# Copies of the value windows in long runs in later blocks, and the transposes of the chunk inverses 22 products later, in a transformer layer on one core

## The chip, the cores and the metric

The kernel runs on one core of a Trainium2 chip. The metric is the device time of one execution in microseconds (us). Before the change the median of 3 runs is 1508.61 us (1508.04 to 1511.2).

## The reference

One layer of a diffusion backbone: 1024 latent tokens and 256 context tokens, width 1024. After modulation and RMS norm, one input projection feeds two groups of heads: a gated DeltaNet (group A, 4 heads of 128, scanned forward and backward) and a neighbourhood attention (group B, 8 heads of 64, windows of 8 rows by 32 gathered columns on a grid of 64 columns). Both go through an output projection and a SwiGLU feed-forward. What matters here:

```python
# group A: q, k, v of the short convolution; one chunk of the scan needs the inverse of a unit triangle
m = jnp.where(strict, jnp.einsum("bhncd,bhnmd->bhncm", kb, k) * decay, 0.0)
a_mat = jnp.eye(CHUNK, dtype=f32) + m
u = lax.linalg.triangular_solve(a_mat, v * beta[..., None], left_side=True, lower=True, unit_diagonal=True)
w = lax.linalg.triangular_solve(a_mat, kb * jnp.exp(gam)[..., None], left_side=True, lower=True, unit_diagonal=True)
...
# group B: normalised queries and keys, values of a window of columns
q = rms_norm(q, q_norm_w) * NA_HEAD_DIM ** -0.5
k = rms_norm(k, k_norm_w)
...
v_r = lax.dynamic_slice_in_dim(vg, r0, win_rows, axis=1)[:, :, key_cols]
```

## The kernel before

Every number is kept as a pair of a rounded value and its rest (hh and hl for the activations, whi and wlo for the weights), and a product of two such pairs is three matmuls on TensorE (PE). The input projection is computed in blocks of 128 columns. The list `jobs` holds them in order: k0 to k3 and a wide block; from `inv` on nk0, nk1, nk2, a wide block, nk3 (keys of group B); nq0, nq1, nq2 (its queries), q0; from `turn` on q1, q2, q3 (queries of group A), v0 to v3, nq3; from `gates` on z0 to z3. A block goes through eight steps k, each with hh by whi, hl by whi and hh by wlo, for two segments of 512 tokens (nq, q, z: 48 products of 128 x 512) or for 256 + 512 + 512 tokens (k, nk, v). Each block has its weights loaded by SyncE (SP) one block ahead (L218), cast to whi by ScalarE (ACT, L219) and subtracted to wlo by GpSimd (POOL, L221); whi and wlo have two buffers, wraw one. At its end ACT evacuates the PSUM banks into `cacc` (L491), of which there are two.

`norm()`, called one block later, does for nk and nq blocks: products of the squares with a block matrix (m<-cr,cst and pr<-cr,cst, L548), Ln and Exp on ACT (L549 to L553, each with a load of its function table), the scaling by VectorE (DVE, L556), a cast to half precision on ACT (L561 for nk, L568 for nq), the subtraction for its rest on DVE (L562, L569), and stores to nk_d or nq_d (L574).

Beside the blocks a generator, `bg`, is stepped once per k before `turn` and three times after. It yields after small pieces of work:

- `block_inverses()` inverts 32 x 32 triangles: a recursion of 60 DVE steps over the matrix N (L947, L949), the diagonal set (L952), one yield, then 32 transposes of N on PE into PSUM banks `m` (written at L957 and recorded at L106, the line of the helper), eight copies from them to WK on DVE (L961), and for both directions a 32 x 32 transpose (L967), a store to x_d, a scaling (L970) and another store (L972).
- `preps()` then makes 20 preparations, one per direction and chunk of 128 tokens, up to three in flight. One loads e, kk and xc (xc from x_d; L997 to L999), copies xc into fx on ACT (L1011) and into y on POOL, takes exponentials of e on ACT (L1015), multiplies kk by e on DVE (L1016), and then does four dependent groups of products on PE: pr<-fx,kk, whose result ACT copies back (L1028), and three of pr<-y,kk, each of which needs the copy on DVE of the one before it (L1036).

A third generator, `copies`, is added after the wide block 8 and stepped twice per k: `windows()` copies the values' columns of four overlapping windows from nv_d to vw_d in DRAM, 16 copies of 256 KB in runs of 2 KB, on SP's queue (L1095). The attention, behind the input projection, loads vw from vw_d (L331).

PE, ACT, DVE, POOL and SP each run their instructions in order. A scheduler decides this order when the program is built, from priorities that follow the program's text and from when operands are ready; it can move an instruction between blocks. Where an engine waits, all that stands behind it in its order waits too.

Of the kernel before, what the change touches and what calls it, by code (L numbers as in the profile page):

```python
# [9 lines left out]
F32 = mybir.dt.float32  # L10
# [4 lines left out]
OP = mybir.AluOpType  # L15
# [12 lines left out]
NU = NCH * NH  # L28
# [63 lines left out]
def hybrid(ctx, tc, a, dbg):  # L92
# [75 lines left out]
    vw_d = dram.tile([128, 4, 4, 512], F32, name="vw_d", tag="vw_d")  # L168
# [130 lines left out]
    def attention(nw):  # L299
# [28 lines left out]
        def values(hp, half, cb):  # L328
            if (hp, cb) not in blocks:
                vw = nw.tile([128, 4, 128], F32, name="vw", tag="vw", bufs=3)  # L330
                sp.dma_start(vw, vw_d[:, cb, :, hp * 128:hp * 128 + 128])  # L331
                blocks[hp, cb] = vw
            return blocks[hp, cb][:, half:half + 3]
# [87 lines left out]
    with ExitStack() as bs:  # L421
# [32 lines left out]
        class Block:  # L454
# [79 lines left out]
            def norm(self):  # L534

                kind, acc, t0, i = self.kind, self.acc, self.t0, self.i
                if kind in "vz":
                    return
                if kind == "k":
                    sp.dma_start(kT_d[:, i], acc)  # L540
                    return
                r = self.r
                if kind == "q":
                    sp.dma_start(qT_d[:, i], acc[:, t0:])
                    return
# [8 lines left out]
                isk = kind == "nk"  # L554
# [332 lines left out]
        def block_inverses():  # L887
            with ExitStack() as gs:
# [75 lines left out]
                for d in range(2):  # L964
                    ud = U[:, d * NU:(d + 1) * NU]
                    ut = g4.tile([128, NU, 32], F32, name="ut", tag="ut")
                    dve.transpose(fl(ut), fl(ud))  # L967
                    x, s = (ut, ud) if d else (ud, ut)
                    sp.dma_start(x_d[:, d, 0], x)
                    dve.tensor_tensor(s, s, NB[:, d].rearrange("p c (h o) -> p (c h) o", o=1).to_broadcast(  # L970
                        [128, NU, 32]), OP.mult)
                    sp.dma_start(x_d[:, d, 1], s)  # L972
                    yield

        done = set()

        def preps():

            first_half.close()
            with ExitStack() as gs:  # L980
# [11 lines left out]
                def fetch(d, c):  # L992
# [6 lines left out]
                    sp.dma_start(xc, x_d[:, d, :, c * 4:c * 4 + 4])  # L999
# [56 lines left out]
                n = 0  # L1056
                while live or todo or landing:
# [27 lines left out]
        values = inv + 3  # L1085
# [5 lines left out]
        def windows():  # L1091
            vlat = nv_d[CT:].rearrange("(r c) d -> r c d", c=64)
            for cb in range(4):
                for ch in range(4):
                    sp.dma_start(vw_d[:, cb, ch], vlat[4 * ch:4 * ch + 4, BLKS[cb]:BLKS[cb] + 32])  # L1095
                    yield
# [12 lines left out]
        first[0].norm()  # L1109
        first[1].silu()  # L1110
        for n in range(2, len(jobs) + 2):
# [28 lines left out]
            if isinstance(j, Wide):  # L1140
                for t, _ in enumerate(j.tiles()):
# [15 lines left out]
            elif j:  # L1157
                for k in range(KT):
# [12 lines left out]
            if isinstance(j, Wide) and n == values:  # L1171
                copies.add(windows())
            if nrm:
                nrm.norm()
# [689 lines left out]
```

## Time and profile before

| what | value |
|---|---|
| median of 3 runs | 1508.61 us |
| the profiled execution | 1507.78 us |
| its span, first to last instruction | 1506.0 us |
| PE busy | 1449.8 us |
| mean granted clock of PE | 0.994 |
| places of nk3's end, nq0, nq1 and nq2 in the span | about 250 to 308 us |

The profile comes from one execution. A row of a timeline has the start in us from the span's start, the duration, the engine, the line, the operation, output and inputs by the program's names, sizes and count; in brackets stands the idle time of the engine before it and what ended that. In the windows each engine's busy time is followed by the count of instructions, then come the granted clock of PE (1.00 is full), the busy share of the DMA engines and GB/s.

### The profile page before, as it was taken

What the parts mean: (1) busy time and instruction counts of PE and PEld (TensorE: products, weight loads), DVE (VectorE), ACT (ScalarE), POOL (GpSimd) and SP (SyncE); (2) the same over time, 40 slices, a digit from 0 to 9 for tenths busy, and PEclk for the clock granted to TensorE, in tenths of its full rate; (3) what the DMA queues carried; (4) which work ended last, traced back from release to release, by engine and by line L of the source; (5) the groups of instructions that cost most, each with busy time, mean ns of one, the idle gap of its engine ahead of it and who ended that gap; (6) DMA issues with size and microseconds to landing.
All of it is one profiled execution on the core that took longest, in us unless ns stands there. A gap on an engine that the chain in (4) does not pass through costs nothing.

```text
span 1506.0 us, 23093 instructions
## 1 busy us (share of the span) xinstructions
PE 1449.8 (96%) x8365; PEld 1201.0 (80%) x8365; DVE 1004.4 (67%) x1892; ACT 696.2 (46%) x1321; POOL 193.4 (13%) x223
## 2 busy tenths in 40 slices
PE   5999998899999999999989999999999999999998
PEld 2789787678877778887877878888888888888887
DVE  4886579455598427679966499666655557698642
ACT  6443461584266526566742374333333334354440
POOL 0154500343124221211100000000000000000000
PEclk9999999999999999999999999999999999999999
DMA  9377133555377799986349106333333334898742
GB/s 368 117 234 239 57 92 121 191 168 190 118 243 238 220 284 265 262 228 193 110 134 332 72 30 203 113 105 105 102 102 105 106 105 161 287 349 286 240 145 84
DMA packets 198851, 267.35 MB, mean 178 GB/s; under 512 B 15232, under 2 KB 106960, under 8 KB 197712
## 3 DMA queue, kind: packets, MB, share of 16 engines
q1 hardware_dynamic: 198016, 265.49, 54.7%
q8 instruction: 66, 1.08, 0.3%
q14 instruction: 49, 0.40, 0.1%
q10 hardware_dynamic: 720, 0.37, 0.1%
HBM read 201.01 MB, written 68.98 MB: 179 GB/s over the span
## 4 chain that ended last, share of the span: by engine, by line
PE 51%; DVE 6%; ACT 3%; DMA 2%; issue 1%; SPq 0%; ACTq 0%; DVEq 0%
PE ps L102 45%; PE sc L102 5%; PE sc L106 2%; DMA wad<-wa 1%; ACT pt L377 1%; ACT ex L365 1%; DVE ex L363 1%; DVE acc L255 1%; DVE x L1618 1%; DVE x L1594 0%; DVE ex L367 0%; DVE ulo L1449 0%; DVE lT L1589 0%; DVE ws L1444 0%; ACT x L1598 0%
## 5 line engine op out<-in xcount | busy, mean ns | idle before, releaser
L102 PE MATMUL ps<-hT,uhi 128*128 128x512 f32 x496 | 146.8, 390 | 0.8 <-DVE e L1739 0.7
L102 PE MATMUL ps<-lT,uhi 128*128 128x512 f32 x496 | 146.4, 389 | 0.0
L102 PE MATMUL ps<-hT,ulo 128*128 128x512 f32 x496 | 146.3, 389 | 0.0
L102 PE MATMUL blk<-hh,whi 128*128 128x512 f32 (+1 forms) x456 | 138.0, 393 | 2.4 <-ACT hh L748 1.7
L102 PE MATMUL blk<-hh,wlo 128*128 128x512 f32 (+1 forms) x456 | 129.7, 377 | 0.0
L102 PE MATMUL ps<-hB,uhi 128*128 128x512 f32 x436 | 129.1, 390 | 0.0
L102 PE MATMUL blk<-hl,whi 128*128 128x512 f32 (+1 forms) x456 | 129.0, 376 | 0.0
L102 PE MATMUL ps<-lB,uhi 128*128 128x512 f32 x436 | 128.8, 389 | 0.0
L102 PE MATMUL ps<-hB,ulo 128*128 128x512 f32 x436 | 128.8, 389 | 0.0
L1448 ACT CAST uhi<-ws 128x512 fp32r<-128x512 f32 x91 | 54.7, 622 | 145.5 <-PE ps L102 78.2
L1448 ACT CAST uhi<-wq 128x512 fp32r<-128x512 f32 x101 | 60.4, 621 | 132.8 <-PE ps L102 69.4
L1449 DVE TENSOR_TENSOR ulo<-wq,uhi 128x512 fp32r<-128x512 f32 x101 | 67.1, 687 | 65.6 <-ACT uhi L1448 36.4
L102 PEld LDWEIGHTS ps<-hT,uhi 128*128 128x128 f32 x496 | 93.0, 188 | 20.7 <-ACT uhi L1448 1.1
L102 PEld LDWEIGHTS ps<-lT,uhi 128*128 128x128 f32 x496 | 93.0, 188 | 19.7 <-DVE lT L1602 0.5
L102 PEld LDWEIGHTS ps<-hT,ulo 128*128 128x128 f32 x496 | 93.1, 188 | 19.4
L102 PEld LDWEIGHTS ps<-hB,uhi 128*128 128x128 f32 x436 | 81.8, 188 | 17.5 <-issue 0.5
L102 PEld LDWEIGHTS ps<-lB,uhi 128*128 128x128 f32 x436 | 81.8, 188 | 17.3 <-DVE lB L1602 0.4
L102 PEld LDWEIGHTS ps<-hB,ulo 128*128 128x128 f32 x436 | 81.8, 188 | 17.0
L102 PEld LDWEIGHTS blk<-hh,wlo 128*128 128x128 f32 x456 | 80.1, 189 | 17.6 <-issue 1.7
L102 PEld LDWEIGHTS blk<-hl,whi 128*128 128x128 f32 x456 | 80.7, 189 | 15.5
L102 PEld LDWEIGHTS blk<-hh,whi 128*128 128x128 f32 x456 | 76.5, 189 | 19.8 <-ACT hh L748 3.7
L1449 DVE TENSOR_TENSOR ulo<-ws,uhi 128x512 fp32r<-128x512 f32 x91 | 60.6, 685 | 36.2 <-ACT uhi L1448 28.0
(341 smaller groups left out, 3026.0 us busy)
## 6 DMA issues: line engine op xcount, KB each, us to landing
wq<-w_fo SPq DMA_DIRECT2D x99, 256.0 KB
wq<-w_gu SPq DMA_DIRECT2D x88, 256.0 KB
wad<-wa SPq DMA_DIRECT2D x64, 256.0 KB
t_d<-g SPq DMA_DIRECT2D x22, 512.0 KB
fr<-t_d SPq DMA_DIRECT2D x44, 256.0 KB
bt<-rpb SPq DMA_DIRECT2D x48, 192.0 KB
f_d<-g SPq DMA_DIRECT2D x33, 256.0 KB
fr<-f_d SPq DMA_DIRECT2D x33, 256.0 KB
```

The costliest lines, as they stand in the source:

```text
L102: i = nc.tensor.matmul(*args, **kw)
L106: i = nc.tensor.transpose(*args, **kw)
L255: dve.scalar_tensor_tensor(acc2, x, sc, acc2, op0=OP.mult, op1=OP.add)
L363: dve.tensor_tensor_reduce(ex, sc, bt, 1.0, -3.0e38, OP.add, OP.max, m[:, 0:1])
L365: act.activation(ex, ex, AF.Exp, bias=m[:, 1:2], accum_out=m[:, 2:3])
L377: act.copy(pt, sc)
L1448: act.copy(hi, self.raw[key])
L1449: dve.tensor_tensor(lo, self.raw[key], hi.bitcast(F32), OP.subtract)
L1618: dve.tensor_tensor(B[at][:, k], B[x][:, k], B.get(y, B["B11"])[:, k], OP.subtract)
```

## The change

Four things are changed.

1. vw_d is laid out by window, and `windows()` makes 4 copies of 1 MB, 16 runs of 64 KB each, in program order, one in each of the blocks q2, q3, v0 and v1 (at k = 4).
2. The inverses' transposes come after eight yields instead of one. They are kept in program order; their copies, both 32 x 32 transposes and both scalings get a higher priority. The buffer `ut` becomes a part of N.
3. `norm()` ends after the Exp and returns its second half (`split`: scaling, cast, subtraction, stores). For nk3 this half is issued behind the inverses' last scaling, after block 11's products; for other blocks before `turn` it is issued behind the inverses as well, once they exist.
4. `preps()` fetches the first two chunks ahead and yields three times, and after `turn` `bg` is stepped four times at k = 7.

The core of the diff:

```diff
-    vw_d = dram.tile([128, 4, 4, 512], F32, name="vw_d", tag="vw_d")
+    vw_d = dram.tile([4, 512, 512], F32, name="vw_d", tag="vw_d")
...
-                sp.dma_start(vw, vw_d[:, cb, :, hp * 128:hp * 128 + 128])
+                sp.dma_start(vw, vw_d[cb].rearrange("(n p) d -> p n d", p=128)[:, :, hp * 128:hp * 128 + 128])
...
-                isk = kind == "nk"
+                return self.split
+
+            def split(self):
+
+                acc, t0, i, r = self.acc, self.t0, self.i, self.r
+                isk = self.kind == "nk"
...
-                for _ in range(1):
+                for _ in range(8):
                     yield
                 U = WK.rearrange("p d u i -> p (d u) i")
                 for i0 in range(0, 32, 4):
                     p = bank()
                     for i in range(4):
-                        pe.transpose(p[:, i * P:(i + 1) * P], N[:P, :, :, i0 + i].rearrange("p b r -> p (b r)"),
-                                     ident[:P, :P])
-                    dve.tensor_copy(U[:, :, i0:i0 + 4], p[:, :4 * P].rearrange("p (i u) -> p u i", i=4))
+                        tc.keep_in_program_order(nc.tensor.transpose(
+                            p[:, i * P:(i + 1) * P], N[:P, :, :, i0 + i].rearrange("p b r -> p (b r)"),
+                            ident[:P, :P]))
+                    with tc.high_priority(offset=400):
+                        dve.tensor_copy(U[:, :, i0:i0 + 4], p[:, :4 * P].rearrange("p (i u) -> p u i", i=4))
...
-                    ut = g4.tile([128, NU, 32], F32, name="ut", tag="ut")
+                        ut = N.rearrange("p b r c -> p (b r c)")[:, d * 1280:(d + 1) * 1280].rearrange(
+                            "p (u i) -> p u i", i=32)
...
+                inverse[:] = [end]
+                yield
...
+                landing += [[fetch(*todo.pop(0)), False] for _ in range(2)]
+                for _ in range(3):
+                    yield
...
-                for ch in range(4):
-                    sp.dma_start(vw_d[:, cb, ch], vlat[4 * ch:4 * ch + 4, BLKS[cb]:BLKS[cb] + 32])
-                    yield
+                tc.keep_in_program_order(nc.sync.dma_start(
+                    vw_d[cb].rearrange("(r c) d -> r (c d)", c=32),
+                    vlat[:, BLKS[cb]:BLKS[cb] + 32].rearrange("r c d -> r (c d)")))
+                yield
...
-                    bg.step(1 if n < turn else 3)
+                    bg.step(1 if n < turn else 4 if k == 7 else 3)
                     bg2.step(1)
-                    copies.step(2)
+                    if k == 4:
+                        copies.step(1)
+                if waiting:
+                    while not started:
+                        bg.step(1)
+                    with tc.issue_after(inverse[0].ins):
+                        waiting.pop()()
                 j.evac()
...
-            if isinstance(j, Wide) and n == values:
+            if n == turn:
                 copies.add(windows())
             if nrm:
-                nrm.norm()
+                rest = nrm.norm()
+                if nrm is tail and not inverse:
+                    waiting.append(rest)
+                else:
+                    with tc.issue_after(inverse[0].ins) if inverse and n < turn else ExitStack():
+                        rest()
```

The order on the engines, at the three places that the prediction speaks of. First PE at the transposes (m<-cst,N). Before, they stand in block nq0, from its 33rd product on, among single products (numbers behind hh, hl are those of the activations' tiles; what a row waits for stands in brackets):

```order
L102 MATMUL blk<-hh_417,wlo 128x512 x2
L102 MATMUL blk<-hh_419,whi 128x512 x2
L106 MATMUL m<-cst,N 128x80 [waits DVE_49]
L106 MATMUL m<-cst,N 128x80
L102 MATMUL blk<-hl_420,whi 128x512 x2
L102 MATMUL blk<-hh_419,wlo 128x512
```

After, they stand in the next block, nq1, behind its first six products (tiles 136 and 137 are a block's first):

```order
L102 MATMUL blk<-hh_136,whi 128x512 x2
L102 MATMUL blk<-hl_137,whi 128x512 x2
L102 MATMUL blk<-hh_136,wlo 128x512 [waits Pool_49]
L102 MATMUL blk<-hh_136,wlo 128x512
L964 MATMUL m<-cst,N 128x80 [waits DVE_49,Activation_49]
L964 MATMUL m<-cst,N 128x80
L964 MATMUL m<-cst,N 128x80 [waits DVE_49]
L964 MATMUL m<-cst,N 128x80
```

The last 16 products of nq0, nk3's norm products and six products of nq1 now stand ahead of the first transpose; the rest of the transposes follows in groups of eight with six products between. The first preparation's product (pr<-fx,kk) moves in the same way, in block nq2, from behind 26 products to behind 42.

Second, ACT ahead of the first preparation (fx<-xc). Before, from the Exp of nk3 on:

```order
L553 ACTIVATE cr<-cr 128x1280 [waits Activation_49]
L561 CAST hl_2526<-cacc 128x1280 [waits DVE_49]
L219 CAST whi<-wraw 128x1024 [waits DMAHW3_49,PE_49,Pool_49]
L491 ACTIVATE cacc<-blk 128x512 [waits DVE_49,PE_49]
L491 ACTIVATE cacc<-blk 128x512 [waits PE_49]
L549 ACT_TABLE_LOAD
L549 ACTIVATE cr<-m,bias 128x512 [waits PE_49] x2
L532 ACTIVATE cr<-cacc 128x1024 [waits Activation_49]
L551 ACT_TABLE_LOAD
L551 ACTIVATE cr<-cr,bias 128x1024 [waits Activation_49]
L1011 COPY fx_2478<-xc 32x4x32 [waits DMAHW2_49,Pool_49]
```

After, from the same Exp on (lines are five higher here and ten higher from L1006 on):

```order
L553 ACTIVATE cr<-cr 128x1280 [waits Activation_49]
L219 CAST whi<-wraw 128x1024 [waits DMAHW2_49,PE_49,Pool_49]
L549 ACT_TABLE_LOAD
L549 ACTIVATE cr<-m,bias 128x512 [waits PE_49] x2
L551 ACT_TABLE_LOAD
L551 ACTIVATE cr<-cr,bias 128x1024 [waits Activation_49]
L566 CAST hl_2552<-cacc 128x1280 [waits DVE_49]
L573 CAST hl_2570<-cacc 128x512 [waits DMAHW6_49,DMAHW5_49,DMAHW7_49,DMAHW4_49,DVE_49]
L573 CAST hl_2570<-cacc 128x512
L491 ACTIVATE cacc<-blk 128x512 [waits DVE_49]
L491 ACTIVATE cacc<-blk 128x512
L1021 COPY fx_2519<-xc 32x4x32 [waits DMAHW4_49,DMAHW5_49,DMAHW0_49,Pool_49]
```

The cast of nk3 (hl_2526 before, hl_2552 after) moves behind the Ln and Exp of nq0, and nq0's own casts and the evacuation of nq1 stand ahead of the copies into fx.

Third, PE between q3 and v0. Before, v0 follows on q3 at once:

```order
L102 MATMUL blk<-hl_424,whi 128x512 x2
L102 MATMUL blk<-hh_423,wlo 128x512 x2
L102 MATMUL blk<-hh_136,whi 128x256 [waits Activation_49]
L102 MATMUL blk<-hh_136,whi 128x512 [waits Activation_49]
L102 MATMUL blk<-hl_137,whi 128x256
```

After, three preparations stand between them, of which these are the first rows (y_2515 and fx_2519 are one preparation's tiles, y_2516 and fx_2520 the next one's):

```order
L102 MATMUL blk<-hl_424,whi 128x512 x2
L102 MATMUL blk<-hh_423,wlo 128x512 x2
L102 MATMUL pr<-fx_2519,kk 128x96 x4
L102 MATMUL pr<-y_2515,kk 32x32 [waits Activation_49]
L102 MATMUL pr<-y_2515,kk 32x32 x3
L102 MATMUL pr<-fx_2520,kk 128x96 [waits PE_49]
L102 MATMUL pr<-fx_2520,kk 128x96 x3
L102 MATMUL pr<-y_2515,kk 32x64 [waits DVE_49]
L102 MATMUL pr<-y_2515,kk 32x64 x3
L102 MATMUL pr<-y_2516,kk 32x32 [waits Activation_49]
L102 MATMUL pr<-y_2516,kk 32x32 x3
```

The twelve groups of three preparations, which before lie among the products of v2, are moved three blocks ahead and stand together.

More of the change, by code (lines that the diff above doesn't have):

```diff
@@ L537, in norm @@
                 if kind in "vz":
-                    return
+                    return int
                 if kind == "k":
                     sp.dma_start(kT_d[:, i], acc)
-                    return
+                    return int
                 r = self.r
@@ L544, in norm @@
                     sp.dma_start(qT_d[:, i], acc[:, t0:])
-                    return
+                    return int
                 for s0, n in self.segs:
@@ L958, in block_inverses @@
                     for i in range(4):
-                        pe.transpose(p[:, i * P:(i + 1) * P], N[:P, :, :, i0 + i].rearrange("p b r -> p (b r)"),
-                                     ident[:P, :P])
-                    dve.tensor_copy(U[:, :, i0:i0 + 4], p[:, :4 * P].rearrange("p (i u) -> p u i", i=4))
+                        tc.keep_in_program_order(nc.tensor.transpose(
[3 more added lines that the diff above has]
+                        dve.tensor_copy(U[:, :, i0:i0 + 4], p[:, :4 * P].rearrange("p (i u) -> p u i", i=4))
                     if i0 % 8 == 4:
                         yield
-                for d in range(2):
-                    ud = U[:, d * NU:(d + 1) * NU]
-                    ut = g4.tile([128, NU, 32], F32, name="ut", tag="ut")
[L967 to L972, printed above, removed]
-                    yield
-        done = set()
+                with tc.high_priority(offset=400):
+                    for d in range(2):
+                        ud = U[:, d * NU:(d + 1) * NU]
+                        ut = N.rearrange("p b r c -> p (b r c)")[:, d * 1280:(d + 1) * 1280].rearrange(
+                            "p (u i) -> p u i", i=32)
+                        dve.transpose(fl(ut), fl(ud))
+                        x, s = (ut, ud) if d else (ud, ut)
+                        sp.dma_start(x_d[:, d, 0], x)
+                        end = dve.tensor_tensor(s, s, NB[:, d].rearrange("p c (h o) -> p (c h) o", o=1).to_broadcast(
+                            [128, NU, 32]), OP.mult)
+                        sp.dma_start(x_d[:, d, 1], s)
+                inverse[:] = [end]
+                yield
+        done, inverse, waiting, started = set(), [], [], []
         def preps():
@@ L998, in fetch @@
                     sp.dma_start(kk, kk_d[:, c])
-                    sp.dma_start(xc, x_d[:, d, :, c * 4:c * 4 + 4])
+                    started.append(sp.dma_start(xc, x_d[:, d, :, c * 4:c * 4 + 4]))
                     at = None
@@ L1084, in hybrid @@
         later = len(jobs)
-        values = inv + 3
+        tail = jobs[inv + 4]
         queries = range(turn - 1, later)
@@ L1108, in hybrid @@
         first[1].evac()
-        first[0].norm()
+        first[0].norm()()
         first[1].silu()
@@ L1145, in hybrid @@
                     if t == 4 and nrm:
-                        nrm.norm()
+                        nrm.norm()()
                         for _ in fin:
@@ L1170, in hybrid @@
             done.add(n - 2)
-            if isinstance(j, Wide) and n == values:
+            if n == turn:
                 copies.add(windows())
             if nrm:
-                nrm.norm()
+                rest = nrm.norm()
[4 more added lines that the diff above has]
+                        rest()
             if isinstance(j, Block) and j.later is None:
```

1 line of the change is left out of this document (removed).

## The prediction

> **What bounds the kernel now.** I read the page first, then the waits of PE, then the granted clock by windows, and last the timelines of single engines around the two long waits. The page says who the bottleneck is:
>
> ```profile
> span 1506.0 us, 23093 instructions
> PE 1449.8 (96%) x8365; PEld 1201.0 (80%) x8365; DVE 1004.4 (67%) x1892; ACT 696.2 (46%) x1321; POOL 193.4 (13%) x223
> ```
>
> PE (TensorE) idles 56 us in all, so an edit that changes no product can gain only idle time or clock. The waits of PE from 200 to 560 us, where all of the edited code runs (who waited for whom: us in total, times, longest):
>
> ```profile
> PE pr L102 <- DVE kk L1016: 6.9, 1, 6.9
> PE m L106 <- DVE N L952: 5.4, 1, 5.4
> ...
> PE pr L102 <- DVE y L1036: 1.2, 2, 0.8
> ```
>
> The first two are single waits: the first preparation product (pr<-fx,kk) and the first transpose of the inverses (m<-cst,N). The third says that the twenty preparations, which all lie behind them, cost PE only 1.2 us more. Windows (PE, PEld, DVE, ACT and POOL busy, granted clock, DMA share, GB/s) add the price in clock:
>
> ```profile
> 254.00:264.00 10.00, 4.58 (x19) 3.44 (x18) 8.69 (x16) 0.00 (x0) 0.00 (x0) 0.78 0.26 94
> 264.00:268.00 4.00, 4.00 (x24) 3.56 (x23) 1.98 (x5) 0.00 (x0) 0.00 (x0) 0.69 0.61 201
> ...
> 300.00:305.00 5.00, 5.00 (x28) 3.90 (x28) 2.19 (x4) 3.23 (x9) 3.80 (x10) 0.60 0.72 228
> ...
> 376.00:414.00 38.00, 38.00 (x226) 33.15 (x225) 22.92 (x37) 10.88 (x17) 5.31 (x3) 1.00 0.38 115
> ```
>
> With a clock of one half or one, .78 over 10 us is 4.4 us at half, ending in the next window, and .69 over 4 us is 2.5 us more; .60 over 5 us is 4 us. The timeline of PE (start, duration, operation, count, idle before and its releaser) gives the work in it:
>
> ```profile
> 262.41 0.53 PE L106 MATMUL m<-cst,N 80*128 80x80 f32 x2 [5.42 <-DVE N L952]
> ...
> 284.37 1.88 PE L102 MATMUL m<-cr,cst 128*128 128x512 f32 x4
> 285.69 1.04 PE L102 MATMUL blk<-hh,whi 128*128 128x512 f32 x2
> 286.56 0.62 PE L102 MATMUL blk<-hl,whi 128*128 128x512 f32 x2
> ...
> 291.57 0.61 PE L102 MATMUL blk<-hh,whi 128*128 128x512 f32 x2
> 299.09 2.02 PE L102 MATMUL pr<-fx,kk 128*128 128x96 f32 x8 [6.90 <-DVE kk L1016]
> ```
>
> First dip: PE works from 262.41 to 266.5 at half speed, 4.1 us that would have taken 2.0. Second: from 299.09 to 304.0, 4.9 us that would have taken 2.5. The two places cost 5.4 + 2.0 + 6.9 + 2.5 = 16.8 us. From 286.56 to 291.57 stand 22 products: 0.228 us each.
>
> **The transposes, 22 products later.** They wait for the recursion on DVE, whose last steps are:
>
> ```profile
> 249.47 0.98 DVE L949 TENSOR_TENSOR N<-N,tt 80x792 f32<-80x792 f32 x1
> 250.49 3.02 DVE L947 TENSOR_TENSOR tt<-N 80x736 f32<-80x736 f32 x1
> ...
> 262.93 0.28 DVE L949 TENSOR_TENSOR N<-N,tt 80x120 f32<-80x120 f32 x1
> ...
> 305.62 0.42 DVE L1036 COPY y<-pr 32x256 f32<-32x256 f32 x1 [0.20 <-PE pr L102]
> ```
>
> The recursion ends at 263.2. PE stopped at 257.0; now it first runs 16 more products of nq0 (3.6 us), the norm products of nk3 (284.37 to 285.69 is 1.3 us for two segments of 512; nk3 has two and a half: 1.65) and 6 products of nq1 (1.4), so it arrives at 263.7. Of 5.4 us nothing would be left. But one of these DVE rows took 3.02 us instead of about 0.98, and a POOL subtraction lay beside it:
>
> ```profile
> 250.07 2.66 POOL L221 TENSOR_TENSOR wlo<-wraw,whi 128x1024 fp32r<-128x1024 f32 x1 [44.72 <-ACT whi L219]
> ```
>
> The next such subtraction, for nq2's weights, waits for a load that SP issues only behind the vw_d copies:
>
> ```profile
> 249.66 11.61 SPq L1095 DMA_DIRECT2D vw_d<-nv_d  x5
> 261.36 2.26 SPq L218 DMA_DIRECT2D wraw<-w_nqk  x1
> ```
>
> The copies go from this stage, so the load can be issued at 252.7, when the subtraction at 250.07 frees its buffer, 8.7 us earlier. Its cast on ACT then waits for nq0's last product, whose weight buffer it takes, and this is now at 260.6. So the POOL subtraction falls at about 261.6 to 264.2, on the recursion's last steps. If it blocks DVE as at 250.49, the recursion ends 3.02 - 0.98 = 2.0 us later and PE stalls 1.6. The Trainium skill, "SBUF — State Buffer", section "SBUF: two separate sides", says that a VectorE instruction with two SBUF inputs and a GpSimd one that reads SBUF take a shared port pair in turn, for the whole instruction; the row at 250.49 agrees, and this speaks against the change. By the rule in full the stall is 1.6, without it near 0. From the rows alone the bounds are 0 and 2.0 (DVE's delay in full); I take 1.3, since the overlap is probable, and no dip. Gain: 5.4 - 1.3 + 2.0 = 6.1 us. nq1 then ends at about 278 instead of 284.37.
>
> **The first preparation.** Before, it was ready 14.7 us after nq1's last product (299.09 - 284.37), by a chain on ACT:
>
> ```profile
> 283.62 1.26 ACT L561 CAST hl<-cacc 128x1280 f16<-128x1280 f32 x1 [1.62 <-DVE cacc L556]
> ...
> 286.50 1.09 ACT L491 ACTIVATE cacc<-blk 128x512 f32<-128x512 f32 x2 [0.67 <-DVE hl L562]
> 287.61 1.28 ACT L549 ACT_TABLE_LOAD   x1
> ...
> 295.35 1.25 ACT L1011 COPY fx<-xc 32x128 f32<-32x128 f32 x4 [1.77 <-DMA xc<-x_d]
> ...
> 301.84 1.14 ACT L568 CAST hl<-cacc 128x512 f16<-128x512 f32 x2
> ```
>
> Now nk3's second norm half stands behind the scalings, and in ACT's order nq0's Ln and Exp come first, then nk3's cast (1.26), nq0's casts (1.14), the evacuation of nq1, the copies into fx and the exponentials. From 14.7 go the wait for xc (1.8: the scalings end before the chain gets there), the table load (1.3, it can precede nq1's end) and 0.7 of the lead at 286.50; the two casts add 2.4 and DVE's subtraction, for which the evacuation waits, about 0.5. That is 13.8. PE now reaches the preparation after 42 products of nq2 instead of 26: 16 x 0.228 = 3.6 later, 11.4 after nq1's end (before: 299.09 - 6.90 - 284.37 = 7.8). The stall is 2.4 us; with a chain not shortened at all 3.3, with casts off the chain 0. I take 2.5. A 3.3 us wait elsewhere, for the output projection's weights, left the clock alone, for behind it two products take 0.63 us, as at 286.56:
>
> ```profile
> 780.16 0.74 PE L102 MATMUL sc<-gah,whi 128*128 128x512 f32 x2 [3.30 <-ACT whi L219]
> 780.75 0.63 PE L102 MATMUL sc<-gal,whi 128*128 128x512 f32 x2
> ```
>
> So no dip. The Trainium skill, "TensorE: Matmul & The Clock Gate", section "Why this matters for your kernels", asks for no PE idle gaps over about 3 us, one idle window being enough to halve the clock; this row stands against its plain figure. By that rule a stall of 3.3 would still cost some 1.7 us more. Gain: 6.9 - 2.5 + 2.5 = 6.9, less about 0.6 for the next two preparation steps, which now follow with 6 products between them: 6.3.
>
> **Preparations in rows of their own.** The third preparation's exponentials now stand on ACT behind nq1's norm, two table loads and two activations (1.28 each by the row at 287.61): I estimate 2.5 us of PE wait in q0, between 0 and 5. Further on PE's order has five places without a block product in between: the 12 dependent groups of three preparations, which before lay among the products of v2, in one row between q3 and v0; and some 24 more, transposes among them, in four places from v2's end to z0's. A group waits for the copy of the one before it: by the row at 305.62 the copy takes 0.42 and starts 0.20 behind PE's end, so a group with no cover loses up to 0.62 us; groups of different preparations cover one another. 36 groups: 0 to 22 us. The nearest row is the 1.2 us that all the preparations lost before, but those had products between them; I take 0.18 each, 6.5, against 1.2 that goes: 5.3 more.
>
> **The copies in runs of 64 KB.** In nk3 they held SP for over 20 us, not PE; their going is in the first term. Now each is 1 MB, one per block from q2 on. In the window 376 to 414 DMA was .38 busy at 115 GB/s: the rest, 188 GB/s, moves 2 MB (read and write) in 11 us, about a block's length. Weights are loaded a block ahead, so I take 0; if each delays a weight load by a whole 5 us, 20. The other edits (two outputs in N, 1 yield for 2) issue the same instructions: 0.
>
> **Sum.** 6.1 + 6.3 - 2.5 - 5.3 = 4.6 us. The profiled execution took 1507.78 (span 1506.0 and 1.8 around it), 0.8 under the median of the runs: it becomes 1503.2, the median 1504.0.
>
> **Rivals.** (a) The cover holds: the late groups overlap as before and q0's wait is short; gain 10 to 12, 1497 to 1499. For it speaks that three preparations are always in flight; against, that nothing else stands between their groups. Chance 0.20. (b) The late groups run as chains: at 0.50 us a group they cost 18, gain 12.4 - 2.5 - 16.8, that is 7 slower, 1515.5; it decides from 0.39 us a group (3 us slower). For it, the waits on DVE or ACT in nearly every group; against, that before only 1.2 us were lost. Chance 0.12. (c) The second stall only moves: nk3's second half and the casts hold ACT so that the preparation is ready as late after nq1 as PE is early; 6.9 us and the dip stay, less the late losses: 6.1 - 7.8, 1510. Chance 0.13. (d) The gate closes on the stall that is left, by the rule above: 1.7 worse than the forecast, 1505.7; chance 0.15. The forecast itself has 0.40.
>
> **The numbers.** The forecast is 1504.0. The range reaches from (a), 1498, to (c) with 1 us over it, 1511; (b) and the tail of (a) are left out. A measurement can tell 0.2%, 3.0 us: under 1505.6 is faster, over 1511.6 slower. Faster: 0.20 of (a), 0.33 of the forecast, 0.05 of (d): 0.58. Slower: (b) and a part of (c), 0.15. Same: 0.27.
>
> **What would show it.** In the waits of PE after the change: the transposes' first wait under 2 us (right) or over 4 (wrong); the first preparation's 2 to 3.5 with the clock at 1.0; the sum of waits for y and kk between 345 and 530 about 6 us (0 to 2: rival a; over 15: rival b); q0's wait for fx about 2.5; a POOL subtraction beside a long last step of the recursion. Wrong altogether would be a block's whi that waits for wraw behind a copy of 1 MB.

## The result and the profile after

| kernel | median us | against before | 95% interval |
|---|---|---|---|
| before | 1509.13 | | |
| after, three of four runs | 1562.57 | 1.0354 | 1.0326 to 1.0382 |
| after, run again (after_again) | 1560.74 | 1.0350 | 1.0329 to 1.0371 |

The change makes the kernel 3.5% slower, some 53 us, where 4.6 us faster was forecast. One of the four runs, the profiled one, had a mean granted clock of 0.652 and took 2107.76 us (the others 1560.02 to 1565.89), so it is left out of the median and the profile shown here is that of after_again. A ratio, here and below, is against the runs of before made beside the kernel in question (for after_again their median is 1507.59 us). The page of after_again and its waits of PE from 150 to 640 us:

```profile
span 1558.1 us, 23103 instructions
PE 1461.8 (94%) x8365; PEld 1209.5 (78%) x8365; DVE 998.3 (64%) x1892; ACT 696.4 (45%) x1320; POOL 192.8 (12%) x223
```

```profile
PE blk L102 <- ACT whi L219: 26.6, 4, 22.2
PE m L106 <- ACT cacc L529: 8.5, 1, 8.5
PE pr L102 <- DVE kk L1026: 7.5, 7, 2.5
PE pr L102 <- ACT kk L1038: 4.7, 3, 3.5
PE pr L102 <- DVE y L1046: 4.5, 6, 1.9
...
PE m L964 <- DVE N L957: 0.4, 1, 0.4
PE m L964 <- DVE N L954: 0.3, 1, 0.3
```

The two long waits that the change was about are gone: the transposes wait 0.4 and 0.3 us (before: 5.4), the first preparation 2.5 (before: 6.9). In their place PE waits 26.6 us for blocks' weights (whi) and 8.5 for an activation that transposes of v2 read (cacc L529).

To see where the time goes, the start of each block's first product in the timeline of PE, counted from the first product of nq0, can be set against the same in before. Negative is ahead of before (us):

| from nq0 to | q0 | q2 | v0 | z0 | z3 |
|---|---|---|---|---|---|
| before, us | 65.9 | 94.8 | 123.9 | 232.9 | 286.7 |
| after_again | -16.1 | -4.6 | +3.4 | +24.6 | +53.8 |
| copies_only | -4.5 | -4.5 | +6.4 | +19.3 | +59.0 |
| old_copies | -1.6 | +9.9 | +9.9 | +9.5 | +9.5 |
| z_first | -16.1 | -4.6 | +3.5 | +25.3 | +28.7 |
| copies_unpinned | -0.3 | +5.8 | +9.6 | +17.4 | +16.3 |
| copies_early | +15.4 | +32.7 | +37.4 | +36.9 | +37.0 |
| extra_tiny | +15.7 | +33.2 | +35.2 | +36.8 | +36.8 |
| extra_flat | +15.7 | +33.3 | +34.4 | +35.2 | +34.9 |
| extra_full | +17.5 | +34.3 | +32.7 | +66.8 | +98.1 |
| runs_16x4 | -16.1 | -4.6 | +10.7 | +28.2 | +28.7 |
| runs_16x16 | -16.1 | -4.2 | +3.6 | +21.1 | +21.6 |
| copies_pool | -16.1 | -4.9 | -4.9 | +16.3 | +15.8 |
| no_copies | -17.6 | -6.1 | -6.1 | -6.6 | -6.5 |
| before_no_copies | -4.5 | -4.5 | -4.5 | -5.0 | -5.0 |
| nc_wait1 | -4.6 | -1.1 | -1.1 | -1.5 | -1.4 |
| nc_move | -11.5 | -0.5 | -0.5 | -0.6 | -0.6 |
| nc_no_fetch | -14.3 | -5.7 | -4.9 | -4.8 | -4.7 |

At q0 and q1 much of a row's lead is work put off: preparations that before lie in nq2 now lie in q0 and q1. At q2 the first four preparations are done in all kernels, so q2 is the first fair mark. At v0 the row can again show moved work (after_again has twelve groups of preparations between q3 and v0, copies_only eleven, no_copies none). So the changed kernel wins 4.6 us by q2 and loses 58 behind it, 29 of these from z0 to z3. The 4.6 must be read beside copies_only and before_no_copies: both have the transposes, the norm and the preparations of before and differ from it, up to q2, in that nk3 is free of the old copies; both win 4.5 by q2. The waits of before_no_copies show how:

```profile
PE m L106 <- DVE N L954: 5.4, 1, 5.4
PE pr L102 <- DVE kk L1018: 3.3, 1, 3.3
```

The transposes wait as long as in before, but the first preparation waits 3.3 us in place of 6.9, on the same order of ACT up to there. So most of what the changed kernel wins by q2 comes with the copies' leaving nk3.

**A weight load behind a store, a cast behind an evacuation.** SP's timeline around the start of block v0:

```profile
356.20 0.54 SPq L1107 DMA_DIRECT2D vw_d<-nv_d  x1
380.07 0.56 SPq L629 DMA_DIRECT2D qk_d<-kk  x1
380.72 0.62 SPq L544 DMA_DIRECT2D qT_d<-cacc  x1
381.44 1.05 SPq L218 DMA_DIRECT2D wraw<-w_conv  x1
```

SP stands 23 us at the store of qk_d, whose data ACT writes late, and the load of the weights of v1 is queued behind it: it is issued at 381.44, 15 us ahead of v1's first product, where before it is issued at 362.01, 29 us ahead. Then ACT, which casts the weights of v1 (first after_again, at the start of v1, then before, at the start of v0):

```profile
393.68 1.35 ACT L506 COPY cr<-blk 128x256 f32<-128x256 f32 x3 [5.57 <-PE blk L102]
394.91 1.07 ACT L219 CAST whi<-wraw 128x1024 fp32r<-128x1024 f32 x1
```

```profile
372.99 1.05 ACT L219 CAST whi<-wraw 128x1024 fp32r<-128x1024 f32 x1 [1.75 <-PE blk L102]
373.95 1.07 ACT L506 COPY cr<-blk 128x512 f32<-128x512 f32 x2
```

Before, the cast of v1's weights runs a whole block ahead, ahead of the evacuation (L506) there, and v1 starts at once. After, it stands behind the evacuation of v0, and PE waits 1.9 us at v1 and 2.0 at v2, the latter with a dip. The row at 394.91 has no wait of its own: the load landed at 388.9, while ACT waited for PE. So these 3.9 us are the place of the cast in ACT's order, not a late load; that the plan puts the cast there because the load stands behind the store is likely, but not shown. At v3 the cast stands behind an activation that waits for DVE's convolution, and in PE's order v2's transposes, which need that activation, stand ahead of v3 (8.5 us and a dip):

```profile
443.87 1.27 ACT L529 ACTIVATE cacc<-cacc 128x1280 f32<-128x1280 f32 x1 [8.17 <-DVE cacc L520]
445.04 1.03 ACT L219 CAST whi<-wraw 128x1024 fp32r<-128x1024 f32 x1
```

**A weight load behind the attention's loads.** SP and ACT ahead of z2 in after_again, then SP in before:

```profile
553.72 0.32 SPq L1062 DMA_DIRECT2D y_d<-y  x1
554.09 0.57 SPq L279 DMA_DIRECT2D kT<-kT_d  x1
...
568.73 0.58 SPq L218 DMA_DIRECT2D wraw<-w_z  x1
```

```profile
574.85 1.04 ACT L219 CAST whi<-wraw 128x1024 fp32r<-128x1024 f32 x1 [20.25 <-DMA wraw<-w_z]
```

```profile
520.22 0.59 SPq L218 DMA_DIRECT2D wraw<-w_z  x1
520.90 0.68 SPq L279 DMA_DIRECT2D kT<-kT_d  x1
```

The last preparation's store comes at 553.72, the attention's first loads follow, and only then the weights: PE waits 22.2 us. Before, the weights go first.

### The profile page after: what moved, and what is told of

It reads as the page before. It is cut to its first block, busy times and chain, and to the rows that moved or that the text cites. A ratio compares the mean times of both kernels' runs of the same rounds, so it can differ in the third digit from the quotient of the medians.

```text
span 2105.9 us, 23103 instructions
## 1 busy us (share of the span) xinstructions
PE 2040.0 (97%) x8365; PEld 1426.4 (68%) x8365; DVE 995.2 (47%) x1892; ACT 704.8 (33%) x1320; POOL 187.2 (9%) x223
## 4 chain that ended last, share of the span: by engine, by line
PE 63%; DMA 0%; DVE 0%; ACT 0%; issue 0%; SPq 0%; ACTq 0%
PE ps L102 54%; PE sc L102 7%; PE sc L106 2%; PE ps L106 0%; DMA wraw<-w_out 0%; ACT pt L377 0%; DVE ex L363 0%; DVE x L1522 0%; DVE z L1318 0%; DVE xa L1815 0%; ACT ex L365 0%; ACT whi L219 0%; SPq L218 0%; SPq L1445 0%; ACTq L219 0%
## 5 line engine op out<-in xcount | busy, mean ns | idle before, releaser
L102 PE MATMUL blk<-hh,whi 128*128 128x512 f32 (+1 forms) x456 | 178.3, 498 | 28.1 <-ACT whi L219 27.0
L102 PE MATMUL ps<-hT,ulo 128*128 128x512 f32 x496 | 199.7, 507 | 0.0
L102 PE MATMUL ps<-lT,uhi 128*128 128x512 f32 x496 | 199.4, 507 | 0.0
L102 PE MATMUL ps<-hT,uhi 128*128 128x512 f32 x496 | 199.4, 506 | 0.0
L102 PE MATMUL ps<-hB,uhi 128*128 128x512 f32 x436 | 176.1, 508 | 0.0
L102 PE MATMUL ps<-lB,uhi 128*128 128x512 f32 x436 | 175.7, 508 | 0.0
L102 PE MATMUL ps<-hB,ulo 128*128 128x512 f32 x436 | 175.4, 506 | 0.0
L102 PE MATMUL blk<-hh,wlo 128*128 128x512 f32 (+1 forms) x456 | 170.6, 480 | 1.4 <-POOL wlo L221 1.4
L102 PE MATMUL blk<-hl,whi 128*128 128x512 f32 (+1 forms) x456 | 169.6, 480 | 0.0
L102 PEld LDWEIGHTS blk<-hh,whi 128*128 128x128 f32 x456 | 92.1, 219 | 67.8 <-ACT whi L219 28.8
L102 PEld LDWEIGHTS ps<-hB,ulo 128*128 128x128 f32 x436 | 90.4, 207 | 51.9 <-issue 16.3
```

What stands on the lines that cost most here:

```text
L102: i = nc.tensor.matmul(*args, **kw)
```

## The experiments

Three theories are told apart: the **order** that is planned around the copies and their hold in program order; the **transfer** itself holding the DMA engines; the **preparations** in rows of their own.

**after_again** is the changed kernel once more.

> The changed kernel once more, for an undisturbed profile. Order theory: the copies of 1 MB are held in program order on SP, so that weight loads are no longer moved ahead of them, and the planned order of the casts and loads behind them is worse. Then 1560 to 1566 us, with PE waiting 20 to 30 us once for the weights of a z block (w_z is issued behind the attention's first loads) and at each of the ends of q3 to v3 for a cast of weights that stands behind an evacuation on ACT. Transfer theory: the copies themselves hold the DMA engines; then the waits for whi begin while a copy is under way, with a DMA share near 1.0 in that wait. Preparation theory: the preparations in rows of their own cost it; then the waits for y and kk sum to over 30 us.

1560.74 us, as the order theory had it: 22.2 us for w_z and waits for casts at v1, v2 and v3. The waits for y and kk sum to 16.7 us, not over 30. The DMA engines, in forty slices of 1.75 us from 350 to 420, busy tenths and GB/s:

```profile
DMA  0099995000000000019999600000199995000000
GB/s 0 4 299 295 335 711 228 0 0 0 9 0 0 0 0 0 0 31 315 266 329 647 294 0 0 0 0 0 34 317 264 345 676 236 9 0 0 0 0 0
```

The view counts a packet whole in the slice in which it begins, so 711, 647 and 676 GB/s are not rates. Two windows show it (DMA share and GB/s are the last two numbers):

```profile
360.00:361.00 1.00, 1.00 (x9) 0.99 (x9) 0.80 (x2) 0.28 (x1) 0.00 (x0) 1.00 2.81 1166
361.00:364.00 3.00, 3.00 (x14) 2.44 (x13) 0.06 (x1) 1.84 (x2) 0.00 (x0) 1.00 0.00 0
```

A share of 2.81 in 1 us is 2.8 us of all engines, most of it one copy of 1 MB. Then the engines stand idle for some 9 us or more. The waits for weights at v1 and v2 (394 and 414) fall into idle slices, and the waits of 8.5 and 22.2 us begin 33 and 150 us after the issue of the last copy (403.29). The copies land 8.2 us after their issue (median), those ahead of v1 and v2 issued at 384.06 and 403.29, so no copy is under way in any of these four waits.

**copies_only**: the kernel before with the new copies alone.

```diff
+    vw_d = dram.tile([4, 512, 512], F32, name="vw_d", tag="vw_d")
+                tc.keep_in_program_order(nc.sync.dma_start(
+                    vw_d[cb].rearrange("(r c) d -> r (c d)", c=32),
...
-            if isinstance(j, Wide) and n == values:
+            if n == turn:
                 copies.add(windows())
```

> The kernel before with the new copies alone (layout of vw_d, 4 copies of 64 KB runs in program order, one per block from q2 on); transposes, norm and preparations as before. Order theory and transfer theory: 1550 to 1575 us, nearly all of the 55 us. Preparation theory: within 5 us of before, 1505 to 1515.

1567.13 us, 1.0392 (1.0377 to 1.0408). The whole loss comes with the copies. Here too three preparations stand between q3 and v0, so these rows come with the copies and not with the other edits; the waits for y and kk sum to 14.4 us (before: 8.4, 6.9 of them at the first preparation), which leaves the theory of the preparations a small part at most.

**old_copies**: the changed kernel with the old 16 copies in nk3.

```diff
-                tc.keep_in_program_order(nc.sync.dma_start(
+                for ch in range(4):
+                    sp.dma_start(vw_d[:, cb, ch], vlat[4 * ch:4 * ch + 4, BLKS[cb]:BLKS[cb] + 32])
...
-            if n == turn:
+            if isinstance(j, Wide) and n == inv + 3:
```

> The changed kernel with the old copies (16 of 256 KB in runs of 2 KB, from block nk3 on); all else as changed. Order and transfer theory: what the prediction gave for the other parts, 1498 to 1508 us. Preparation theory: over 1545.

1520.37 us, 1.0081 (1.0066 to 1.0097): a miss of all theories, which gave it a gain or a large loss. With SP full of old copies the rest of the change costs 13 us, most of it in one place:

```profile
PE m L964 <- ACT cr L549: 13.4, 1, 13.4
```

```profile
275.16 1.04 ACT L219 CAST whi<-wraw 128x1024 fp32r<-128x1024 f32 x1 [21.12 <-DMA wraw<-w_nqk]
276.11 1.08 ACT L491 ACTIVATE cacc<-blk 128x512 f32<-128x512 f32 x2
277.21 1.28 ACT L549 ACT_TABLE_LOAD   x1
278.50 1.05 ACT L549 ACTIVATE cr<-m,bias 128x256 f32<-128x256 f32 x2
```

The transposes, now behind nk3's norm products, need PSUM banks that ACT frees with Ln (L549); Ln stands behind a cast that waits for weights; and SP issues this load behind the vw_d copies. The transposes' new place needs the copies to go from nk3.

**z_first**: the changed kernel, weights of the last z blocks first.

```diff
             if n + 1 < len(jobs):
-                jobs[n + 1].prefetch()
+                with tc.high_priority(offset=2000) if n > gates else ExitStack():
+                    jobs[n + 1].prefetch()
```

> The changed kernel, with a higher priority for the loads and casts of the weights of the last two z blocks, so that they stand ahead of the attention's loads on SP; copies as changed. Order theory: the wait of some 23 us for w_z goes, 1530 to 1545 us, and the casts behind evacuations stay. Transfer theory: 1555 to 1566, since the copies are unchanged.

1540.51 us, 1.0211 (1.0180 to 1.0243). The table shows it: equal to after_again up to z0, then +3.4 instead of +29.2. With the copies unchanged, 26 us of the loss in the z blocks go by the place of two blocks' loads and casts alone. In the whole kernel 20 us go; where the rest is lost again behind z3 was not traced.

**copies_early, copies_unpinned, extra_full, extra_tiny.** The first adds the four long copies in nk3 to nq2, the second only drops the hold. The other two are copies_early with copies that nobody reads, held in program order at the places of the change (1 MB, or 64 KB).

```diff
 # copies_early
-            if n == turn:
+            if isinstance(j, Wide) and n == inv + 3:
                 copies.add(windows())
 # copies_unpinned
-                tc.keep_in_program_order(nc.sync.dma_start(
+                sp.dma_start(
 # extra_full (extra_tiny: [:, 0:1024] on both sides)
+                tc.keep_in_program_order(nc.sync.dma_start(
+                    ex_d[cb].rearrange("(r c) d -> r (c d)", c=32),
+                    vlat[:, BLKS[cb]:BLKS[cb] + 32].rearrange("r c d -> r (c d)")))
```

> The changed kernel with its four copies of 1 MB from block nk3 on (one per block to nq2) instead of from q2 on; all else as changed. The planned order of casts and weight loads behind q1 is then that of the kernel before. Order theory: the 58 us lost behind q2 go, and the early gain stays, 1498 to 1507 us against 1507.6 before. Transfer theory: the copies then hold weight loads in nk3 to nq2 instead, 1515 to 1560. Rival for the early part: the 11 us that the preparations give back in q0 and q1 stay in any case, and the whole is within 3 us of before.

> The changed kernel without the hold in program order on the four copies, which the scheduler then places itself (two ahead of nq0, two among the q blocks). Order theory: 1498 to 1512 us. Transfer theory: two of the four copies still run among the loads of the q blocks, so about half of the loss stays, 1525 to 1545.

> copies_early with four more copies of 1 MB into a buffer that nobody reads, held in program order, one per block from q2 on as in the changed kernel. They serve nothing and nothing waits for their data. Order and transfer theory: most of the loss comes back, 1540 to 1570 us. If it stays under 1515, neither the place nor the size of these copies is the cause, but what waits for vw_d.

> The same with extra copies of 64 KB (16 runs of 4 KB) in place of 1 MB, held in program order at the same places. The planned order behind q1 is then nearly that of copies_early, weight loads of z ahead of the attention's loads. If the hold alone is the cause, 1540 us or more. If the cause is the order that the scheduler plans around long copies, within 4 us of copies_early.

copies_early took 1547.49 us, 1.0246 (1.0219 to 1.0273): the loss behind q2 is nearly gone (+32.7 to +37.0), as the order theory said, but ahead of q2 it is 33 us behind before and 37 behind after_again, where that theory had expected no loss; the transfer theory's range fits the sum. Here, too, an order shows: SP issues two copies at 239.14, then nothing until the inverses' store at 272.42, and only behind the inverses' four stores, at 278.55, the load of nq2's weights, which after_again issues at 252.31. copies_unpinned: 1526.77, 1.0110 (1.0083 to 1.0137), in the range of the transfer theory. extra_full: 1603.92, 1.0620 (1.0587 to 1.0652), above the range of both theories, since copies_early was already slow: copies that nobody waits for bring the loss back, 64 us from q2 to z3. extra_tiny: 1548.43, equal to copies_early: the hold alone, on copies of 64 KB, does nothing. So long copies cost wherever they stand, and these four times by themselves leave both theories open.

**extra_flat and extra_eighth** tell them apart. extra_flat moves 1 MB four times as extra_full does, but from one piece of nv_d; extra_eighth moves an eighth of extra_full's bytes. The instructions of these two stand in the same order on every engine, another one than in extra_full.

```diff
 # extra_flat
-                    ex_d[cb].rearrange("(r c) d -> r (c d)", c=32),
-                    vlat[:, BLKS[cb]:BLKS[cb] + 32].rearrange("r c d -> r (c d)")))
+                    ex_d[cb].rearrange("(r s c) d -> (r s) (c d)", s=8, c=4),
+                    nv_d[CT:CT + 512].rearrange("(r c) d -> r (c d)", c=4)))
 # extra_eighth: [:, 0:2048] on both sides of extra_full's copy
```

> As extra_full, four extra copies of 1 MB in program order that nobody reads, but from a piece of nv_d that lies in one run instead of 16 rows apart: the same bytes and 16 pieces of 64 KB at the same places. The order planned for it is another, on all engines the one of extra_eighth. Order theory: within 5 us of copies_early (1547). Transfer theory: as extra_full, 1590 to 1610.

> As extra_full with an eighth of the bytes (16 runs of 8 KB). Its order on every engine is that of extra_flat, which moves eight times as much. Order theory: equal to extra_flat within 3 us. Transfer theory: extra_flat is slower by over 20 us.

1541.86 us and 1542.32 (1.0219 both): eight times the bytes change nothing, and both lie 62 us under extra_full, which moves as many bytes as extra_flat. Nor is a copy from one piece the quicker transfer: the extra copies land 8.0 us after their issue in extra_flat and 7.6 in extra_full (medians). The longest waits of PE from 150 to 660, extra_full and then extra_flat:

```profile
PE blk L102 <- ACT whi L220: 37.6, 7, 23.1
PE pr L102 <- DVE kk L1027: 12.8, 3, 6.5
PE m L102 <- ACT cr L533: 12.8, 3, 8.2
PE m L106 <- ACT cacc L530: 8.5, 1, 8.5
```

```profile
PE m L102 <- ACT cr L533: 12.2, 3, 8.2
PE blk L102 <- ACT whi L220: 7.8, 2, 6.7
PE pr L102 <- DVE kk L1027: 6.5, 1, 6.5
```

The changed kernel's two longest waits (22.2 and 8.5 us there, 23.1 and 8.5 here) are in the first and not in the second. So the loss does not come from the bytes, but from the order of the other instructions that comes with such a copy. Why the scheduler plans so around it was not tried; it may take a long copy from rows that lie apart to last much longer than it does.

**runs_16x4 and runs_16x16**: the changed kernel with its copies in 16 parts of 256 KB, four runs of 64 KB or 16 of 16 KB each, one per k in q2 and q3.

```diff
 # runs_16x4
-                    vw_d[cb].rearrange("(r c) d -> r (c d)", c=32),
+                    vw_d[cb, 128 * s:128 * s + 128].rearrange("(r c) d -> r (c d)", c=32),
-                    vlat[:, BLKS[cb]:BLKS[cb] + 32].rearrange("r c d -> r (c d)")))
+                    vlat[4 * s:4 * s + 4, BLKS[cb]:BLKS[cb] + 32].rearrange("r c d -> r (c d)")))
 # runs_16x16
-                    vw_d[cb].rearrange("(r c) d -> r (c d)", c=32),
+                    vw_d[cb].rearrange("(r c) d -> r (c d)", c=32)[:, 4096 * s:4096 * s + 4096],
 # both
-                    if k == 4:
-                        copies.step(1)
+                    copies.step(1)
```

> The changed kernel with its copies in 16 parts of 256 KB, four runs of 64 KB each, in program order, one per k in q2 and q3; the same bytes in the same runs. The order ahead of q2 is that of the changed kernel, and behind it the loads of z stand ahead of the attention's again. Order theory: the loss behind q2 goes, the 4.6 us won by q2 stay: 1500 to 1506. Transfer theory: 1540 to 1565.

> The same with 16 parts of 16 runs of 16 KB. Order theory: 1500 to 1506, within 2 us of runs_16x4. Transfer theory: 1540 to 1565.

1540.29 us (1.0202, 1.0187 to 1.0218) and 1530.47 (1.0142, 1.0128 to 1.0156): both far outside the order theory's range, the first at the edge of the transfer theory's, the second between the two. The z blocks are right again, but in q3 to v1 the held copies keep a weight load behind the same store (runs_16x4):

```profile
336.83 1.73 SPq L1108 DMA_DIRECT2D vw_d<-nv_d  x3
370.66 0.59 SPq L629 DMA_DIRECT2D qk_d<-kk  x1
371.30 1.79 SPq L1108 DMA_DIRECT2D vw_d<-nv_d  x2
373.18 0.38 SPq L544 DMA_DIRECT2D qT_d<-cacc  x1
373.67 0.61 SPq L218 DMA_DIRECT2D wraw<-w_conv  x1
```

PE waits 13.0 us at v0 and 13.4 at v1. At v0 it has stopped at 371.74, two us before the load is issued at all, and the cast comes at 383.64. The load lands 9.9 us after its issue; in no_copies the load of this block lands after 4.1. So here the transfers have a share too: nearly 6 us of the 13 can be put down to the traffic around a load that is already late.

**no_copies, before_no_copies, nc_wait1, copies_pool.** The first two load vw straight from nv_d, in four loads of 64 KB, and have no copy; nc_wait1 puts the transposes back by one number; copies_pool issues the changed kernel's copies from POOL's queue.

```diff
 # no_copies, before_no_copies
-                sp.dma_start(vw, vw_d[cb].rearrange("(n p) d -> p n d", p=128)[:, :, hp * 128:hp * 128 + 128])
+                src = nv_d[CT:].rearrange("(n r c) d -> r c n d", r=4, c=64)
+                for r in range(4):
+                    sp.dma_start(vw[32 * r:32 * r + 32], src[r, BLKS[cb]:BLKS[cb] + 32, :, hp * 128:hp * 128 + 128])
...
-                copies.add(windows())
 # nc_wait1 = no_copies and
-                for _ in range(8):
+                for _ in range(1):
 # copies_pool
-                tc.keep_in_program_order(nc.sync.dma_start(
+                tc.keep_in_program_order(nc.gpsimd.dma_start(
```

> The changed kernel without any copy: vw is loaded straight from nv_d, in four loads of 64 KB (512 B runs as before) in place of one of 256 KB, so SP issues 48 loads more, spread over the attention. The order up to q1 is that of the changed kernel, and no weight load stands behind a copy. Order theory, in which only the copies hurt and the other parts win 4.6 us by q2: 1500 to 1506 us, against 1508 before. If the other parts lose too behind q2, 1510 or more.

> The kernel before without any copy, vw loaded straight from nv_d in four loads. It shows what the copies' place in nk3 costs before: their 25 us of SP time delay one load of weights. Since that delay is hidden behind the long waits before, within 4 us of before, 1504 to 1511. If it is 1500 or less, the old copies and not the transposes' place made the two long waits.

> no_copies with one yield ahead of the transposes in place of eight: they stand in nq0 again, all else as in no_copies. The wait for the recursion comes back (5.4 us and a dip of 2.0 us): 5 to 8 us slower than no_copies. If it is equal to no_copies, the transposes' new place wins nothing, and the wait only moved.

> The changed kernel with its four copies of 1 MB at the same places, held in program order, but issued from the queue of POOL in place of SP's. SP's order is then free of them. If the hold on SP's queue is the cause, 1500 to 1515. If the order that the planning makes around long copies is the cause wherever they are issued, over 1525; POOL's own order then holds wlo behind them.

no_copies: 1509.08 us, 0.9988 (0.9977 to 0.9999), between its two cases, and the only kernel of all whose interval lies under 1, by 0.1%. By z3 it has won 6.5 us, of which some 4 are lost again behind it. The 48 further loads lie there and are the likely cause; part of it is a wait for the output projection's weights, 4.27 us where before waits 3.30. before_no_copies: 1508.98, 0.9993 (0.9980 to 1.0006), as expected, with 5.0 us won by z3. In the whole time the two can't be told apart, so the other parts of the change are not shown to win anything there; by q2 they are 1.6 us ahead. nc_wait1: 1513.88, 1.0018 (1.0008 to 1.0028): 4.8 us slower than no_copies, so beside the other parts the transposes' place does win about 5 us. copies_pool: 1524.01, 1.0084 (1.0069 to 1.0099), just under its second case: off SP's queue the z blocks lose nothing, but 21 us from v0 to z0 stay, the 8.5 us for cacc among them. The hold on SP is not the whole cause.

**nc_move and nc_no_fetch**: before_no_copies with the second part of the change alone, and no_copies without the early loads of the preparations.

```diff
 # nc_no_fetch = no_copies and
-                landing += [[fetch(*todo.pop(0)), False] for _ in range(2)]
-                for _ in range(3):
-                    yield
```

> The kernel before without copies (vw straight from nv_d) and with the second part of the change alone: transposes after eight yields and in program order, their copies, the 32 x 32 transposes and the scalings at a higher priority. The split of the norm and the preparations' early loads are left as before. If the transposes' place wins 5 us and the other two parts lose 3.6 again, 5 us less than before_no_copies by q2 and 1503 to 1507 in all. If the place wins only together with the split of the norm, equal to before_no_copies or slower.

> no_copies without the early loads and the three yields of the preparations (fourth part of the change). If these put the preparations where they wait for nq1's norm (3.5 us and a dip in q1), the wait shrinks and it is 2 to 5 us faster than no_copies. If the split of the norm makes that wait, it is equal to no_copies.

nc_move: 1512.89 us, 1.0002 (0.9986 to 1.0018); nc_no_fetch: 1510.36, 0.9993 (0.9978 to 1.0008). At q2 nc_move stands at -0.5 and before_no_copies at -4.5: the place alone loses 4.0, the second of its two cases. With the split of the norm (nc_no_fetch) it stands at -5.7. The split is thus worth 5.2 us beside the new place, and the place 5.0 beside the split (no_copies against nc_wait1); either without the other loses 3.4 to 4.0 by q2 (the 3.4 with the early loads in it). The early loads change 0.4 by q2 and 1.8 by z3.

## Why the prediction was wrong, point by point

**The step that failed** is "The copies in runs of 64 KB ... Weights are loaded a block ahead, so I take 0". It priced the transfer and left out what the copies move. The transfer is shorter than estimated (at most 2.8 us of all DMA engines, where 11 beside other traffic were assumed), and extra_flat against extra_eighth shows that its bytes cost nothing there. But with the copies the weight loads stand behind a store on SP, the casts behind the evacuation on ACT, and w_z behind the attention's loads: +58 us behind q2, 34.6 of them in the four waits of 1.9, 2.0, 8.5 and 22.2 us. The prediction read the order of the engines at three places around the transposes and preparations, and not SP's order around the copies themselves, where the store qk_d stands ahead of wraw, nor the last weight loads. The range took in a delay of weights only as a bound that was left out; no rival had this mechanism. The last sign of being wrong came close: a block's whi did wait for wraw, 22.2 us, but behind the attention's loads and not behind a copy.

The sentence before it failed too: "In nk3 they held SP for over 20 us, not PE; their going is in the first term." The copies' going alone wins 4.5 us by q2 (copies_only, before_no_copies), at the first preparation and not at the transposes. That the changed kernel's 4.6 by q2 equals the 4.6 of the forecast's sum is luck.

**The transposes** (gain 6.1 forecast): right at their own place. The wait is 0.4 + 0.3 us, no dip there, so 6.7 of 5.4 + 2.0 are won. The POOL subtraction falls on the recursion's tail as worked out (261.6 to 264.2 forecast), DVE in after_again and then POOL:

```profile
260.74 0.50 DVE L954 TENSOR_TENSOR N<-N,tt 80x336 f32<-80x336 f32 x1
261.28 2.47 DVE L952 TENSOR_TENSOR tt<-N 80x232 f32<-80x232 f32 x1
```

```profile
260.90 2.59 POOL L221 TENSOR_TENSOR wlo<-wraw,whi 128x1024 fp32r<-128x1024 f32 x1 [8.62 <-ACT whi L219]
```

A DVE step of 0.40 us before takes 2.47 and ends 0.3 us behind POOL's. This agrees with the lock of the Trainium skill, "SBUF — State Buffer", section "SBUF: two separate sides".

**The first preparation** (stall 2.5 forecast): 2.48 measured, the chain's sum was right. Its "no dip" was not. The windows of after_again before and after that wait:

```profile
289.00:292.00 3.00, 0.52 (x4) 0.10 (x2) 0.69 (x1) 2.92 (x11) 1.91 (x6) 1.00 0.84 212
292.00:297.00 5.00, 5.00 (x28) 4.00 (x29) 0.98 (x2) 2.94 (x8) 1.35 (x4) 0.66 0.94 270
```

0.66 over 5 us is 3.4 us at half clock, 1.7 us lost, after an idle time of 2.48. That is rival (d)'s price, at a stall shorter than the 3.3 that left the clock alone in before; in no_copies the same stall made no dip in nq2. By the rule that the prediction weighed (the Trainium skill, "TensorE: Matmul & The Clock Gate", section "Why this matters for your kernels": no gaps over about 3 us) 2.48 would be safe; in after_again it was not. After waits of 2 to 3.5 us the clock is not settled by the length alone.

**The preparations in q0** (2.5 forecast): a wait of 1.1 us in q0, so this term was too big. But a wait of 3.5 us and a dip of 1.7 follow in q1, 5.2 us for which the sum had no term; together they make 6.3. The "0.6 for the next two preparation steps" doesn't show as a wait. ACT in after_again at the longer wait:

```profile
324.50 1.28 ACT L1025 ACTIVATE e<-e,GN 128x128 f32<-128x128 f32 x4 [0.16 <-POOL e L1054]
327.31 0.98 ACT L1025 ACTIVATE e<-e,GN 128x128 f32<-128x128 f32 x3 [1.52 <-POOL e L1054]
328.20 1.12 ACT L573 CAST hl<-cacc 128x512 f16<-128x512 f32 x2
329.23 0.47 ACT L1038 COPY kk<-pr 128x384 f32<-128x384 f32 x1
```

The copy back for which PE waits stands behind another preparation's exponentials, which wait for POOL, and a norm's casts. By q2 4.6 us are won where 9.9 (6.1 + 6.3 - 2.5) were forecast, and nearly as much without these parts.

**The groups in rows of their own** (5.3 forecast): the 12 groups ahead of v0 lost 1.8 us and no dip, near the 2.2 that 0.18 a group gives. The later ones are mixed with the waits that the copies brought and can't be told apart: from 345 to 530 the waits for y and kk sum to 9.1 us, where about 6 was the sign. These rows come with the copies: in no_copies none stands between q3 and v0, and from 345 to 530 these waits sum to 1.5 us.

## What to carry to other kernels

Where a scheduler plans the order, a moved DMA is priced by what it pushes aside: read its queue around the new place, and the last loads of every stage, and ask for each load what store stands ahead of it. Two edits can each lose alone and win together (the transposes' place and the norm's split, by q2), and one can need a third (the copies gone from nk3); test them in pairs before one is called good or bad. Of this change nothing is shown to be worth keeping: without any copy it wins 0.1%, but the kernel before without copies has the same median (1508.98 us against 1509.08).

## What was not expected of the hardware

A copy of 1 MB from DRAM to DRAM in 16 runs of 64 KB took at most 2.8 us of all DMA engines in after_again (1166 GB/s at a share of 2.81 in the window of 1 us, so about 415 GB/s at full share). The old copies in runs of 2 KB moved 94 GB/s at a share of 0.26 in before (254 to 264), which would be about 360 at full share, so the difference lies mostly in the share.

In after_again an idle time of PE of 2.48 us was followed by 3.4 us at half clock, in no_copies the same idle time was not. In after_again 1.97 us at v2 was followed by a clock of 0.57 from 416 to 420, 1.92 us at v1 by none, and in before 3.30 us by none.
